# One call for an expert's four inner transposes, slot rows computed ahead of the weight splits, and the gated sum of expert rows on TensorE

## The chip, the cores and the metric

The kernel runs on one core of one Trainium2 chip, in one launch. The metric is the device time of a run in microseconds (us). The time before is 3627.87 us, the median of three runs (3625.42 to 3634.18).

## What is computed

Two layers, each: a modulated RMSNorm, an input projection, token mixing (an RWKV-7 scan, a short convolution, a Fourier mix), an output projection with a gated residual, a second RMSNorm, and a mixture of experts with a gated residual. Layer 0 works on 1280 tokens (256 of context, 1024 latent), layer 1 on the 1024 latent tokens alone; the result is the latent stream after a last RMSNorm. The change touches the mixture of experts:

```python
pg = softmax(h @ router_g_w + router_g_b); pg_top, grp = top_k(pg, 1)          # 4 groups
top_l, top_i = top_k((h @ router_e_w + router_e_b) of that group, 2)          # 8 experts in a group
gates = pg_top * softmax(top_l);  eid = grp * 8 + top_i                        # 2 experts for each token
y[slot] = (silu(xb @ exp_gate[e]) * (xb @ exp_up[e])) @ exp_down[e]            # blocks of 128 rows of one expert
out[token] = sum over its 2 experts of gate * y[slot]
x = x + g2 * out;   at the end: rmsnorm(x, final_g)
```

D_MODEL is 1024 and an expert's width 512, so one expert has 6 MB of float32 weights.

## The kernel before

`trace` runs the layers one after the other: input projection (L397), scan, output projection with the router beside it (`router`, L1276 to L1510), then `experts` (L1513) and `combine` (L1710).

**Float32 accuracy out of faster products.** Every operand of a large product is split into a high part and a rest: `split` writes the high part on ACT (L175) and the rest, source minus high part, on DVE (L176), for some pieces on POOL. A product then takes three passes (`PASS`): high by high, high by rest, rest by high.

**Experts.** The 32 experts of a layer follow one another, with up to 128 rows each. For each, six loads of 1 MB (`load`, L1539, on SP, seven buffers `ld`) bring the weights; `cut` splits them into twelve pieces of 128x1024 in `hl` buffers; a gather on POOL (L1527) brings the expert's rows `xg`; `turn` transposes them on TensorE (L1557, four for each half); `up` makes two products, `pR` and `pU` (L1571, 12 instructions in each of four calls); `act` makes `s` out of them (L1576 on ACT, L1577 and L1578 on DVE); `turned` transposes `s` in four pieces of 128x128 into the PSUM tile `pm` (L1586) and splits the result; `down` makes 24 products (L1595); `out` copies to SBUF (L1601) and scatters the rows to `yb` on POOL (L1602). While an expert computes, the next one's pieces are split and its first `up` stands ahead of this one's `turned`; the next but one's first `turn` stands between `turned` and `down`:

```python
act(x)
if n1:
    up(n1, 0)
    cut(n1, 2, 3, pool=3)
    ask()
turned(x)
if n2:
    turn(n2, 0)
down(x)
```

`in_order` (L158) chains all instructions that are traced inside it, engine by engine, into the order in which they are written (SP is left out); outside it a scheduler orders each engine's instructions from its own estimate. In the first experts of a layer some small router work (`late`, L1498 to L1507) is laid between. Rows beyond 128 of an expert are done by a loop behind the 32 (L1682), which runs once in layer 0; so 65 expert blocks are computed in all.

**Slots.** Which token row stands in which slot is gathered on TensorE into `ids` (L1407, L1408). `primary` (L1440) turns that into the gather and scatter rows `gat` and `sca` by `rows` (L1433 to L1438, five small DVE operations). It is called before `experts`, outside `in_order`. The first gather (L1527) needs `gat`.

**Combine.** For each tile of 128 tokens, ten in layer 0 and eight in layer 1, the two expert rows of a token are loaded as `y0` and `y1` (L1734, L1736). ACT scales `y0` by the first gate (L1737), DVE adds `y1` times the second (L1738), POOL multiplies by the modulation row (L1739), DVE adds the residual (L1740). Then come the norm's square sum (L1742), root (L1744) and reciprocal (L1745). In layer 1 the normed tile is stored (L1747, L1748). In layer 0 the tile is stored (L1750), scaled (L1751), and each pair of tiles goes to `norm1`, which transposes it on TensorE (L307), applies the modulation (L310 on ACT, L313 on DVE) and splits it; the next layer's input projection (L397) begins with all pairs.

## Time and profile before

| | |
|---|---|
| median of three runs | 3627.87 us (3625.42 to 3634.18) |
| the profiled execution | 3623.64 us; span on the core 3621.7 us; 1.9 us lie around it |
| mean granted TensorE clock | 0.906 |
| busy share of the span | PE 85%, PEld 67%, DVE 63%, ACT 52%, POOL 33% |
| DMA | 922 MB, mean 255 GB/s |
| experts, layer 0 / layer 1 | from about 1131 to 1815 us / from about 2916 to 3560 us |
| combine, layer 0 / layer 1 | from about 1819 to 1906 us / from about 3563 us to the end |

PE is TensorE's products, PEld its weight loads, DVE VectorE, ACT ScalarE, POOL GpSimd, SP the queue that issues most transfers. A share of busy time is a mean over stages with different limits, so the stages are read apart, by the views of which rows are copied below. A granted clock of 1.00 is 2.4 GHz, one of 0.50 is 1.2 GHz. A DMA share of 1.00 means that the core's 16 DMA engines are busy all the time.

### The profile page before, as it was taken

How to read it: one execution, taken by the hardware profiler on the slowest of the kernel's cores; microseconds unless marked ns; L12 is line 12 of the kernel's file. 1: busy time of each engine (PE TensorE's matmuls, PEld its weight loads, DVE VectorE, ACT ScalarE, POOL GpSimd, SP SyncE). 2: the span in 40 equal slices, each digit the busy share in tenths (PEclk: the TensorE clock that was granted, in tenths of full speed). 3: DMA queues.
4: the chain of work that ended last, by engine and by line, in shares of the span. 5: the costliest groups of instructions: out<-in, count | busy, mean ns of one | idle time of the engine just before them, and what ended most of it. 6: DMA issues, size and time to landing. Idle time of an engine off the chain costs nothing. (4 is left out here: it accounts for less than half of the span.)

```text
span 3621.7 us, 59282 instructions
## 1 busy us (share of the span) xinstructions
PE 3063.4 (85%) x22308; PEld 2426.6 (67%) x22308; DVE 2281.6 (63%) x3543; ACT 1880.5 (52%) x2838; POOL 1178.0 (33%) x1101
## 2 busy tenths in 40 slices
PE   6998788888997999999829988778878978999992
PEld 3776666676686777777616766556666857777772
DVE  4265566134487888888672665652334778888886
ACT  4343433335344777778652434323343467777783
POOL 0037675211221222222140276743113122233323
PEclk8998888899998999999959988778988989999996
DMA  6677888879746899999667578889795488899995
GB/s 241 207 167 173 185 192 181 246 230 315 260 142 243 334 339 338 365 373 363 257 227 258 144 169 181 176 180 252 240 285 167 133 315 317 331 366 364 360 366 205
DMA packets 708060, 922.35 MB, mean 255 GB/s; under 512 B 335074, under 2 KB 561259, under 8 KB 657852
## 3 DMA queue, kind: packets, MB, share of 16 engines
q1 hardware_dynamic: 669456, 871.05, 75.8%
q0 software_dynamic: 38304, 47.49, 3.9%
q8 instruction: 177, 2.90, 0.3%
q14 instruction: 111, 0.91, 0.1%
q10 hardware_dynamic: 12, 0.00, 0.0%
HBM read 726.92 MB, written 203.23 MB: 257 GB/s over the span
## 5 line engine op out<-in xcount | busy, mean ns | idle before, releaser
L176 DVE TENSOR_TENSOR hl<-ld,hl 128x1024 fp32r<-128x1024 f32 x734 | 869.2, 1228 | 54.2 <-ACT hl L175 44.2
L175 ACT ACTIVATE hl<-ld 128x1024 fp32r<-128x1024 f32 x796 | 798.5, 1052 | 38.4 <-PE pR L1571 21.9
L1571 PE MATMUL pR<-hl,wk 128*128 128x512 f32 x1560 | 455.1, 400 | 0.0
L1571 PE MATMUL pU<-hl,wk 128*128 128x512 f32 x1560 | 446.9, 395 | 0.0
L397 PE MATMUL pb<-hh,wh 128*128 128x512 f32 (+1 forms) x1000 | 393.0, 394 | 10.2 <-ACT wh L175 5.4
L397 PE MATMUL pb<-hl,wh 128*128 128x512 f32 (+1 forms) x1000 | 389.1, 390 | 0.0
L397 PE MATMUL pb<-hh,wl 128*128 128x512 f32 (+1 forms) x1000 | 385.4, 386 | 0.0
L1595 PE MATMUL pA<-hl,wk 128*128 128x512 f32 x1560 | 382.9, 401 | 0.5 <-ACT wk L175 0.5
L1571 PEld LDWEIGHTS pU<-hl,wk 128*128 128x128 f32 x1560 | 294.5, 189 | 68.3
L1595 PEld LDWEIGHTS pA<-hl,wk 128*128 128x128 f32 x1560 | 292.7, 191 | 64.0 <-ACT wk L175 0.7
L1571 PEld LDWEIGHTS pR<-hl,wk 128*128 128x128 f32 x1560 | 288.3, 189 | 60.7 <-ACT wk L175 0.3
L176 POOL TENSOR_TENSOR hl<-ld,hl 128x1024 fp32r<-128x1024 f32 x62 | 184.2, 2971 | 422.4 <-ACT hl L175 422.4
L397 PEld LDWEIGHTS pb<-hh,wh 128*128 128x128 f32 x1000 | 200.2, 200 | 76.8 <-issue 14.1
L1602 POOL DMA_INDIRECT yb<-wk,sca x64 | 94.8, 1482 | 468.2 <-ACT wk L1601 452.1
L1276 PE MATMUL pA<-hl,wk 128*128 128x512 f32 x864 | 226.6, 413 | 7.7 <-POOL wk L176 4.0
L397 PEld LDWEIGHTS pb<-hl,wh 128*128 128x128 f32 x1000 | 201.1, 201 | 37.9 <-issue 10.3
L397 PEld LDWEIGHTS pb<-hh,wl 128*128 128x128 f32 x1000 | 200.2, 200 | 35.2 <-issue 4.6
L1100 POOL DMA_DIRECT2D yD<-yt x72 | 58.0, 805 | 433.7 <-ACT yt L1099 391.6
L1276 PEld LDWEIGHTS pA<-hl,wk 128*128 128x128 f32 x864 | 163.0, 195 | 49.2 <-issue 6.0
L1088 DVE TENSOR_TENSOR tm<-pR,ST 128x256 f32<-128x256 f32 x76 | 32.1, 423 | 249.4 <-PE pR L1083 237.4
L175 ACT ACTIVATE wk<-pm 128x256 fp32r<-128x256 f32 (+1 forms) x195 | 88.8, 455 | 185.6 <-PE pm L1586 169.3
L607 POOL TENSOR_TENSOR gt<-gt,tmp 120x30 f32<-120x30 f32 (+14 forms) x240 | 168.3, 701 | 17.7
(425 smaller groups left out, 5389.6 us busy)
## 6 DMA issues: line engine op xcount, KB each, us to landing
ld<-in_exp_gu SPq DMA_DIRECT2D x260, 1024.0 KB
ld<-in_exp_dn SPq DMA_DIRECT2D x130, 1024.0 KB
st<-rlD SPq DMA_DIRECT2D x80, 512.0 KB
wr<-in_w_in SPq DMA_DIRECT2D x46, 512.0 KB
rlD<-ar SPq DMA_DIRECT2D x64, 320.0 KB
rlD<-X SPq DMA_DIRECT2D x64, 320.0 KB
btD<-bt SPq DMA_DIRECT2D x64, 320.0 KB
st<-abD SPq DMA_DIRECT2D x40, 512.0 KB
```

The costliest lines, as they stand in the source:

```text
L175: nc.scalar.activation(hi, src, AF.Copy)
L176: (eng or nc.vector).tensor_tensor(lo, src, hi.bitcast(F32), op=OP.subtract)
L397: mm = nc.tensor.matmul(ps[:, :n], w[:, k, :], h[:, k, c0:c0 + n], start=(k == 0 and i == 0), stop=(k == KD - 1 and i == 2))
L607: eng.tensor_tensor(gt[:, 0:j, j + 1:32], gt[:, 0:j, j + 1:32], tv, op=OP.add)
L1088: nc.vector.tensor_tensor(tm, RS[:, 1], ST[d], op=OP.add)
L1100: nc.gpsimd.dma_start(self.yD[d][:, ch * C:(ch + 1) * C, :], yt.rearrange("q p d -> q (p d)"))
L1276: nc.tensor.matmul(ps, oo[o][:, k, :], w[k][w_][:, fs], start=(k == 0 and q == 0), stop=(k == KD - 1 and q == 2))
L1571: nc.tensor.matmul(o, x.xT[xi][:, kk, :], w[wi][:, k, :], start=(kk == 0 and i == 0), stop=(kk == KD - 1 and i == 2))
L1595: nc.tensor.matmul(x.y[n], x.h[:, hi_, f, :], dw[wi][:, 0, n * 512:(n + 1) * 512], start=(f == 0 and i == 0), stop=(f == 3 and i == 2))
L1602: nc.gpsimd.indirect_dma_start(out=yb, out_offset=bass.IndirectOffsetOnAxis(ap=x.sca, axis=0), in_=o, in_offset=None, bounds_check=2 * T - ...
```

## The change

Four edits. In `turned` all four transposes are issued first and both splits follow. `primary` is called as the first thing inside `in_order`, so that its operations stand where they are written. At the start of the experts the second expert's first `turn` moves behind the first `up`. In `combine` the gate scaling on ACT, the addition on DVE and the multiplication on POOL go; instead ACT writes two diagonal 128x128 matrices with the gates (identity times gate), TensorE forms the gated sum of `y0` and `y1` as float32 products in PSUM (four of 512 columns for a tile, each sum over two diagonals), and DVE multiplies the PSUM tile by the modulation row.

```diff
             pt = pp.tile([P, 4, P], F32, name="pm")
             x.h = self.wk([P, 2, 4, P], F32R)
+            for f in range(4):
+                nc.tensor.transpose(pt[:, f, :], x.s[:, f * P:(f + 1) * P], self.ident)
             for f2 in (slice(0, 2), slice(2, 4)):
-                for f in range(f2.start, f2.stop):
-                    nc.tensor.transpose(pt[:, f, :], x.s[:, f * P:(f + 1) * P], self.ident)
                 self.split(x.h[:, 0, f2], x.h[:, 1, f2], pt[:, f2])
...
         with self.in_order():
+            primary()
             for e in range(3):
                 xs[e] = slot(e)
...
             turn(x, 0)
             turn(x, 1)
-            turn(xs[1], 0)
             up(x, 0)
             cut(x, 6, 7)
             ask()
+            turn(xs[1], 0)
             cut(xs[1], 0)
...
+        pp = self.tc.alloc_tile_pool(name="cmb", bufs=1, space=PSUM, side="right", reuse_waits="tile")
...
-            nc.scalar.activation(y0, y0, AF.Copy, scale=R["gate"][:, t, 0:1])
-            nc.vector.scalar_tensor_tensor(y0, y1, R["gate"][:, t, 1:2], y0, op0=OP.mult, op1=OP.add)
-            nc.gpsimd.tensor_tensor(y0, y0, rw_[w], op=OP.mult)
+
+            dg = sb.tile([P, 512], F32, name="s2", bufs=N2)[:, :2 * P].rearrange("q (c t) -> q c t", c=2)
+            for c in range(2):
+                nc.scalar.activation(dg[:, c], self.ident, AF.Copy, scale=R["gate"][:, t, c:c + 1])
+            ps = pp.tile([P, D], F32, name="sum", bufs=2)
+            for n in range(2):
+                fs = slice(n * 512, (n + 1) * 512)
+                for c, y in enumerate((y0, y1)):
+                    nc.tensor.matmul(ps[:, fs], dg[:, c], y[:, fs], start=c == 0, stop=c == 1)
+            nc.vector.tensor_tensor(y0, ps, rw_[w], op=OP.mult)
             nc.vector.tensor_tensor(xt, xt, y0, op=OP.add)
...
-        primary()
         k.lp.release()
```

How the change moves instructions is seen at three places. In the rows below a line number is that of the kernel the row belongs to, x3 stands for three such instructions in a row, and [waits DVE_49] for a wait on DVE's semaphore (Activation is ACT, DMASW a transfer that POOL issued).

PE, one expert in the middle of layer 0, before: `pm` takes the transposes of `s`, `pl` those of the rows of the expert after next, `pA` the products of `down`.

```order
L1586 MATMUL pm<-ident,s_13605 128x128 [waits DVE_49]
L1586 MATMUL pm<-ident,s_13605 128x128
L1586 MATMUL pm<-ident,s_13605 128x128 [waits DVE_49]
L1586 MATMUL pm<-ident,s_13605 128x128
L1557 MATMUL pl<-ident,xg 128x128 [waits DMASW7_49]
L1557 MATMUL pl<-ident,xg 128x128 x3
L1595 MATMUL pA<-hl,wk 128x512 [waits Activation_49]
L1595 MATMUL pA<-hl,wk 128x512 x11
```

The same place now:

```order
L1585 MATMUL pm<-ident,s_13605 128x128 [waits DVE_49]
L1585 MATMUL pm<-ident,s_13605 128x128 x3
L1557 MATMUL pl<-ident,xg 128x128 [waits DMASW7_49]
L1557 MATMUL pl<-ident,xg 128x128 x3
L1595 MATMUL pA<-hl,wk 128x512 [waits Activation_49]
L1595 MATMUL pA<-hl,wk 128x512 x3
L1595 MATMUL pA<-hl,wk 128x512 [waits DVE_49]
```

The wait for DVE between the second and the third transpose is gone; a wait for DVE stands at the fifth product of `down` instead.

DVE, the start of the experts of layer 0, as a difference (- before, + now): `rt_ids` and the rows up to `sca` are those that the first gather needs, `hl<-ld` the splits of the first expert's weights.

```order
-L176 TENSOR_TENSOR hl<-ld_10635,hl 128x1024
 L1433 TENSOR_SCALAR rt_z<-rt_ids 128x32
 L1435 TENSOR_SCALAR rt_s<-rt_ids 128x32
-L176 TENSOR_TENSOR hl<-ld_10635,hl 128x1024
 L1436 SCALAR_TENSOR_TENSOR rt_z<-rt_z,rt_ids 128x32
-L176 TENSOR_TENSOR hl<-ld_10637,hl 128x1024
 L1437 TENSOR_TENSOR gat<-rt_z,rt_s 128x32
 L1438 CAST sca<-rt_z 128x32
-L176 TENSOR_TENSOR hl<-ld_10637,hl 128x1024
+L176 TENSOR_TENSOR hl<-ld_10633,hl 128x1024 x2
+L176 TENSOR_TENSOR hl<-ld_10635,hl 128x1024 x2
+L176 TENSOR_TENSOR hl<-ld_10637,hl 128x1024 x2
```

The five operations of `rows` stood among six splits, and now stand ahead of all six.

PE, `combine` of layer 0, now: `sum` takes the products through the diagonals (`s`), `n1ps` the transposes of a pair of tiles by `norm1`.

```order
L1747 MATMUL sum<-y_16763,s_16767 128x512
L1747 MATMUL sum<-y_16765,s_16767 128x512
L1747 MATMUL sum<-y_16784,s_16788 128x512
L307 MATMUL n1ps<-ident,y_16651 128x128 x4
L1747 MATMUL sum<-y_16863,s_16867 128x512
L307 MATMUL n1ps<-ident,y_16672 128x128 x4
L307 MATMUL n1ps<-ident,y_16651 128x128
L307 MATMUL n1ps<-ident,y_16672 128x128
```

Before, only the transposes stood here. Now the products of the third tile, the first product of the fourth and the first one of the fifth stand ahead of or among the transposes of the first pair.

## Rows read from the trace of the kernel before

**Rows 1.** Windows: stretch, us, busy us (instructions) per engine, PEclk, DMA share, GB/s.

```profile
3200.00:3300.00 100.00, 95.34 (x446) 77.82 (x445) 86.77 (x91) 80.42 (x102) 36.01 (x17) 1.00 0.95 360
...
1500.00:1600.00 100.00, 95.34 (x440) 76.71 (x439) 85.61 (x89) 79.44 (x100) 27.94 (x17) 1.00 0.96 369
...
3000.00:3100.00 100.00, 90.72 (x421) 73.70 (x420) 88.06 (x122) 73.18 (x92) 26.58 (x14) 0.98 0.86 320
...
1362.00:1368.00 6.00, 6.00 (x30) 4.88 (x29) 5.05 (x9) 5.31 (x6) 2.50 (x2) 1.00 1.01 380
...
1820.00:1905.00 85.00, 22.74 (x80) 13.98 (x80) 68.12 (x88) 48.56 (x98) 37.80 (x19) 0.50 0.64 241
3564.00:3621.00 57.00, 0.00 (x0) 0.00 (x0) 42.22 (x32) 21.32 (x33) 23.20 (x8) 0.50 0.68 258
```

**Rows 2.** Waits of PE in layer 1's experts: us in total, times, longest us.

```profile
PE pm L1586 <- DVE wk L176: 32.3, 32, 1.8
```

**Rows 3.** Timeline, a steady expert of layer 1: start us, us, engine, line, operation [idle before].

```profile
3246.42 0.69 DVE L1577 TENSOR_TENSOR s<-s,pR 128x512 f32<-128x512 f32 x1 [0.16 <-ACT s L1576]
...
3249.02 0.38 PE L1586 MATMUL pm<-ident,s 128*128 128x128 f32 x2
3249.44 0.38 ACT L175 ACTIVATE wk<-pm 128x256 fp32r<-128x256 f32 x1 [1.16 <-PE pm L1586]
3249.86 0.42 DVE L176 TENSOR_TENSOR wk<-pm,wk 128x256 fp32r<-128x256 f32 x1 [0.82 <-ACT wk L175]
...
3250.34 0.44 PE L1586 MATMUL pm<-ident,s 128*128 128x128 f32 x2 [0.93 <-DVE wk L176]
...
3250.61 0.60 PE L1557 MATMUL pl<-ident,xg 128*128 128x128 f32 x4
...
3250.97 1.86 PE L1595 MATMUL pA<-hl,wk 128*128 128x512 f32 x7
```

**Rows 4.** Timeline of POOL: scatters of neighbouring experts, layer 1, then layer 0.

```profile
3200.95 1.59 POOL L1602 DMA_INDIRECT yb<-wk,sca  x1 [6.59 <-ACT wk L1601]
...
3219.94 1.58 POOL L1602 DMA_INDIRECT yb<-wk,sca  x1 [6.66 <-ACT wk L1601]
...
1671.98 1.50 POOL L1602 DMA_INDIRECT yb<-wk,sca  x1 [6.80 <-ACT wk L1601]
...
1691.22 1.51 POOL L1602 DMA_INDIRECT yb<-wk,sca  x1 [6.79 <-ACT wk L1601]
```

**Rows 5.** Timeline, start of layer 0's experts, DVE.

```profile
1131.58 0.18 DVE L1408 TENSOR_TENSOR rt_ids<-rt_ids,pm 128x32 f32<-128x32 f32 x1
...
1135.69 0.18 DVE L1438 CAST sca<-rt_z 128x32 int32<-128x32 f32 x1
```

**Rows 6.** Timeline of PE, start of layer 0's experts.

```profile
1145.43 1.11 PE L1557 MATMUL pl<-ident,xg 128*128 128x128 f32 x4 [15.36 <-DMA xg<-hx,gat]
...
1149.30 1.09 PE L1557 MATMUL pl<-ident,xg 128*128 128x128 f32 x4 [1.90 <-DMA xg<-hx,gat]
1150.04 1.63 PE L1571 MATMUL pR<-hl,wk 128*128 128x512 f32 x3
```

**Rows 7.** Groups of lines in layer 0's combine: busy us, mean ns | idle before.

```profile
L1751 DVE TENSOR_SCALAR y<-wk,r 128x1024 f32<-128x1024 f32 x10 | 15.7, 1567 | 0.1
...
L1738 DVE SCALAR_TENSOR_TENSOR y<-y,gate,y 128x1024 f32<-128x1024 f32 x10 | 14.5, 1447 | 7.3 <-DMA y<-yb 7.3
```

**Rows 8.** Groups of lines in layer 1's combine.

```profile
L1747 DVE SCALAR_TENSOR_TENSOR wk<-wk,r,xg 128x1024 f32<-128x1024 f32 x8 | 16.2, 2030 | 0.3
L1738 DVE SCALAR_TENSOR_TENSOR y<-y,gate,y 128x1024 f32<-128x1024 f32 x8 | 14.2, 1780 | 18.2 <-DMA y<-yb 18.1
```

**Rows 9.** Timeline of DVE in layer 1's combine, its last operation.

```profile
3616.70 1.28 DVE L1747 SCALAR_TENSOR_TENSOR wk<-wk,r,xg 128x1024 f32<-128x1024 f32 x1
```

**Rows 10.** Line L238 by form: float32 products of 512 columns, min/median/max ns.

```profile
L238 PE MATMUL ps<-w,cc x64: 591/902/1057, 13.7 to 41.3; 128*2 128x512 f32 x64
```

**Rows 11.** Window of PE, the first products of layer 0's experts.

```profile
1149.30:1155.00 5.70, 5.70 (x16) 0.50 0.39 155
```

More of the change, by code (lines that the diff above doesn't have):

```diff
@@ L1510, in router, with experts @@
         return route, primary, finish
-    def experts(self, l, hx, yb, R, finish, xmid, t0):
+    def experts(self, l, hx, yb, R, primary, finish, xmid, t0):
         nc, tc, a = self.nc, self.tc, self.a
@@ L1755, in combine @@
                 t0, xs = t + 1, []
+        pp.release()
 def dft(n, scale):
@@ L1906, in trace @@
             k.outproj(l, last, xs[l], xmid, hx, readout, ots, route)
-        primary()
         k.lp.release()
         k.lp = tc.alloc_tile_pool(name="lde", bufs=1, reuse_waits="tile")
-        xts = k.experts(l, hx, yb, R, finish, xmid, 2 if last else 0)
+        xts = k.experts(l, hx, yb, R, primary, finish, xmid, 2 if last else 0)
         k.scp.release()
```

## The prediction

> **What bounds the kernel now.** I read the windows first, to see which engine is full in which stage. In the steady experts PE is busy 95% of the time at a granted clock of 1.00, and the transfers have a share of 0.95 to 0.96 at 360 GB/s (layer 1) and 369 GB/s (layer 0); in the first experts of a layer, where router work is laid between, it is 0.86 and 320 GB/s [rows 1]. So the experts are bound by PE, with the transfers close behind. The two combines are another matter: PE has a clock of 0.50, the transfers stand at 0.64 and 0.68, and DVE is busy 68.1 of 85 us and 42.2 of 57 us [rows 1]; its chain from tile to tile sets the end.
>
> Then the waits, for what PE's idle time is: in layer 1's experts PE waited for DVE at L1586 32 times, once in each expert, 32.3 us in all [rows 2]. Then the timeline of one expert shows the step itself [rows 3]: two transposes at 3249.02, ACT's split at 3249.44, DVE's at 3249.86, and only then, at 3250.34, the other two, though `s` had long been there. The first product of `down` starts at 3250.97, 1.95 us after the first transpose. The period of an expert is 18.99 us in layer 1 (3219.94 - 3200.95) and 19.24 us in layer 0 [rows 4]. Last, the timelines of the two starts and the groups of lines of the two combines [rows 5 to 8].
>
> **The inner transposes.** Four transposes in a row take 0.60 us [rows 3]. Now both splits wait behind them: four transposes, then ACT's split (0.38), with two handovers of some 0.04 (3249.82 to 3249.86 is one): about 1.06 us from the first transpose to the first product of `down`. The transposes of L1557 (0.60) stand on PE meanwhile and end earlier. 1.95 - 1.06 = 0.89 us saved for each expert. If the first split is released after two transposes it starts as before, at 0.42, and ends 0.80 after the first transpose, but the eight transposes keep PE until about 0.9: 1.05 us saved. DVE's rest (0.42) is wanted first by the fifth product, four products of 0.27 (1.86 for seven, [rows 3]) later, so at 2.1; it is there at about 1.5, covered by 0.6 us. I take 0.89 for 65 blocks: **-58 us**; the ends are -68, and, if everything waits on, 0.
>
> What is late next? The transfers. An expert moves 360 x 18.99 = 6.8 MB in layer 1 and 369 x 19.24 = 7.1 MB in layer 0. At the new periods, 18.1 and 18.35, that asks for 378 and 387 GB/s. A window of 6 us shows 380 at a share of 1.01 [rows 1]. With 380 as the most, layer 1 gets through and layer 0 needs 18.68 us, 0.33 us more for each of some 20 steady experts: **+7 us**.
>
> The Trainium skill, on its page "DMA: Bandwidth & Descriptors", Specifications, gives about 358 GB/s as a core's share of the memory. By that figure a layer 1 expert could not be under 19.1 us, and the steady experts would gain nothing. The trace disagrees already, with 369 over 100 us [rows 1].
>
> **The start of the experts.** `ids` is done at 1131.58 and `sca` at 1135.69, with DVE splits between [rows 5]. The five small operations take some 0.18 us at most each, and now follow one another, and `ids` no longer stands behind two splits: `sca` at about 1131.2, some 4.5 us earlier; without the last effect 3.2. The first gather and all behind it move with it, since PE's first `turn` waited 15.36 us for that gather [rows 6]. The six splits that come later on DVE (about 1.2 us each) end at about 1138.6, before PE's first product wants them at 1143. Moving the second `turn` takes its wait (1.90) and its own 0.74 off the front of the first product (from 1149.30 to 1150.04, [rows 6]); the wait is now covered by twelve products. In sum 4 to 7 us a layer; I take 6, twice: **-12 us**. The weight loads are in SP's queue and don't move ahead.
>
> **Combine, layer 0.** On DVE, L1738 goes (14.5 us) and a product with a PSUM tile of 1024 columns comes. Its price is bounded by twice the row for 512 columns, 2 x 0.69 = 1.38 us [rows 3], and by 1.28, the operation from SBUF [rows 9]; I take 1.3: 13 us for ten tiles, so -1.5. POOL's multiplication goes too. Beside it DVE is slow: L1747 takes 2.03 us on average and 1.28 where POOL is idle [rows 8, 9]. If L1751 (1.57 on average, [rows 7]) loses the same 0.75, that is -7.5. ACT trades a pass over 1024 columns for two of 128, and is not what is waited for. Sum **-9 us**; ends -15 and what the products cost.
>
> That is the added work: a tile has four float32 products, and the trace has such products of 512 columns as two records each, 0.59 us at the high clock, 1.06 at the low [rows 10]. Without overlap a tile is 8 x 0.59 = 4.7 us; at the 0.27 spacing of the products of `down` [rows 3] 2.1. I take the middle, 3.4, and 6.8 at the low clock. At the high clock ten tiles are 34 us, beside 22.7 of transposes (at the low clock, [rows 1]) in a stage of 85: hidden. The change puts three tiles' products in a row at the start, and TensorE's first products of the experts ran 5.7 us at 0.50 before the clock rose [rows 11]; so I expect the clock to rise here within the first two tiles.
>
> **Combine, layer 1.** DVE is the chain. L1738 goes (14.2), the PSUM product comes (8 x 1.3 = 10.4), L1747 drops from 2.03 to 1.28, -6 [rows 8, 9], and the addition between them gains a little. DVE falls by 10 to 12 us; the first tile's products, at the low clock, put 6.8 us where DVE's 1.3 stood, but DVE waited 18.1 us for `yb` there [rows 8], and those transfers run on meanwhile. **-10 us**; ends -14 and the case below.
>
> **The sum.** -58 + 7 - 12 - 9 - 10 = -82 us, against the profiled 3623.64: 3541.6. The median of the runs shown stands 4.2 us above that execution, so I forecast **3546 us**. About 0.3%, 11 us, is what a measurement of this kernel can tell from no change.
>
> **Rivals.**
> *The transfers take over.* If each layer can't move more over long stretches than the 360 and 369 GB/s that it shows [rows 1], the 40 steady experts gain nothing, and only the 24 early ones (share 0.86) and the last block keep 0.89: -22 in place of -51, 3575 us. For it: a share of 0.95 leaves little. Against: 380 in the short window. Chance 0.14.
>
> *TensorE stays at the low clock in the combines.* Then layer 0's needs 10 x 6.8 + 23 = 91 us of PE and some 5 for the first data: 96 against 85, +11 in place of -9. Layer 1's needs 8 x 6.8 = 54, and about 13 for the first data and the last tile's norm and store: 67 against 58, +9 in place of -10. 3546 + 39 = 3585 us; for one of the two alone 3566. For it: PE was at 0.50 through both stages, though layer 0's had 22.7 us of transposes [rows 1].
>
> The Trainium skill, "TensorE: Matmul & The Clock Gate", HAM oscillation, speaks against this part of the change: bursts of products with waits for data between them fall back to the low clock each time. By it both combines would be this rival's. The trace bears it out only as far as the 0.50 goes, with no products in either stage. Chance 0.16.
>
> *The wait only moves.* If the first product of `down` waits for DVE's rest as well, or for the second half's split, it starts at about 1.5 or 1.9 after the first transpose in place of 1.06, and the expert keeps some 0.2 us on average of the two: 13 in place of 51, 3584 us. For it: the added wait at the fifth product. Against: 0.6 us of cover. Chance 0.05.
>
> *Slower.* PE takes its instructions in order, and in layer 0's combine the products of the third tile and the first ones of the fourth and fifth now stand ahead of or among the first pair's transposes. If those wait for loads that need buffers which the norm behind the transposes frees, products and norm run one after the other at the low clock: up to 18 x 6.8 = 122 us bare. -58 + 7 - 12 + 122 = +59, 3687 us. It decides from about half of the products bare (63 of 122 us). Against: only the first product of the later tile stands ahead, and `y0` has five buffers. Chance 0.03.
>
> **Chances.** Forecast 0.62; the others as given. All but the last are faster by over 11 us. Faster 0.95, same 0.02, slower 0.03. The range goes down to where the experts save 68, the starts 14 and the combines 15 and 10 with no loss to the transfers, -107 in place of -82, or 3521; since not all come together, 3522. Up it takes in the three rivals that give 3575 to 3585: 3590.
>
> **What would show it.** Right: no idle PE between transposes at L1585 and a first product of `down` about 1.06 us behind the first; periods of 18.1 us in layer 1 and near 18.5 in layer 0, at a share near 1.00; the first gather near 1131.5; the clock over 0.9 in most of both combines, and DVE's operations there at 1.3 us. Wrong: periods unchanged with PE waiting for `hl` splits that wait for `ld`; a clock of 0.50 in the combines, with DVE waiting for `sum`; or combines longer than 86 and 58 us.

## The result, and the profile after

The change takes the kernel from 3626.64 us (median of 4 runs, 3623.01 to 3634.18) to **3517.65 us** (median of 4, 3517.36 to 3518.51): a ratio of 0.9697, with a 95% interval of 0.968 to 0.9714. The profiled span falls from 3621.7 to 3515.6 us, the mean granted clock rises from 0.906 to 0.926. Faster, as forecast, but by 109 us where 82 were forecast, and 4 us below the range.

To see where the time came from, I cut both spans at the same events: the last product of L1407 (the slots), the first of L1571 (the experts), the first load of `y0`, the first of L397 in layer 1.

| stage, us | forecast | before | after | difference |
|---|---|---|---|---|
| start and layer 0 up to its slots | 0 | 1129.7 | 1132.2 | +2.5 |
| slots to first expert, layer 0 | -6 | 20.3 | 12.8 | -7.5 |
| experts, layer 0 | with layer 1's | 669.5 | 647.4 | -22.1 |
| experts, layer 1 | -51 for both | 628.3 | 610.6 | -17.7 |
| combine, layer 0 | -9 | 86.2 | 76.5 | -9.7 |
| layer 1, first L397 to last L1407 | 0 | 1008.9 | 972.3 | **-36.6** |
| slots to first expert, layer 1 | -6 | 20.3 | 12.8 | -7.5 |
| combine, layer 1 | -10 | 58.5 | 51.0 | -7.5 |
| sum | -82 | 3621.7 | 3515.6 | -106.1 |

The six edited stages gave 72.0 us of the 82 forecast (7.5 + 22.1 + 17.7 + 9.7 + 7.5 + 7.5). A third of the gain, 36.6 us, came in the middle of layer 1, where no line was edited: input projection, scan, Fourier mix, output projection, router.

First the windows of the changed kernel, as in [rows 1]: stretch, us, busy us (instructions) of PE, PEld, DVE, ACT and POOL, granted clock, DMA share, GB/s. The stretches are steady experts of layer 1 and of layer 0, early experts, and the two combines.

```profile
3200.00:3300.00 100.00, 99.78 (x465) 81.38 (x464) 88.81 (x94) 83.38 (x107) 35.72 (x17) 1.00 0.98 377
...
1500.00:1600.00 100.00, 99.82 (x458) 80.33 (x457) 88.92 (x93) 80.99 (x104) 36.15 (x17) 1.00 0.99 385
2900.00:3000.00 100.00, 93.38 (x423) 75.18 (x422) 92.11 (x120) 72.29 (x93) 25.11 (x15) 0.97 0.87 320
1792.40:1868.00 75.60, 56.17 (x158) 26.59 (x158) 54.54 (x89) 43.84 (x106) 7.94 (x8) 0.84 0.73 271
3468.00:3515.00 47.00, 31.77 (x64) 12.68 (x64) 29.76 (x32) 16.34 (x37) 0.00 (x0) 0.86 0.78 297
```

In the steady experts PE is busy 99.8% where it was 95.3%: its wait is gone, and the transfers followed, at 377 and 385 GB/s. In the early experts the transfer rate is 320 GB/s as before: nothing was gained there. The combines have a clock of 0.84 and 0.86 where it was 0.50.

The step itself, in a steady expert of layer 1 (timeline: start us, us, engine, line, operation, idle before), answers to [rows 3]:

```profile
3253.72 0.60 PE L1585 MATMUL pm<-ident,s 128*128 128x128 f32 x4
3254.15 0.60 PE L1557 MATMUL pl<-ident,xg 128*128 128x128 f32 x4
3254.35 0.38 ACT L175 ACTIVATE wk<-pm 128x256 fp32r<-128x256 f32 x1 [1.38 <-PE pm L1585]
3254.77 0.42 DVE L176 TENSOR_TENSOR wk<-pm,wk 128x256 fp32r<-128x256 f32 x1 [1.04 <-ACT wk L175]
3254.79 5.77 PE L1595 MATMUL pA<-hl,wk 128*128 128x512 f32 x24
```

ACT starts at 3254.35, after all four transposes and not after two; the first product of `down` stands 1.07 us behind the first transpose (1.06 forecast), and all 24 run through. The scatters give the period [rows 4]: two of layer 1, then two of layer 0.

```profile
3207.69 1.64 POOL L1602 DMA_INDIRECT yb<-wk,sca  x1 [6.12 <-ACT wk L1601]
...
3225.82 1.65 POOL L1602 DMA_INDIRECT yb<-wk,sca  x1 [6.12 <-ACT wk L1601]
...
1611.12 1.63 POOL L1602 DMA_INDIRECT yb<-wk,sca  x1 [6.19 <-ACT wk L1601]
...
1629.52 1.65 POOL L1602 DMA_INDIRECT yb<-wk,sca  x1 [6.18 <-ACT wk L1601]
```

18.13 us (18.99 before) and 18.40 (19.24): 0.86 and 0.84 a block, 0.89 forecast.

The start of layer 0's experts, DVE [rows 5] and PE [rows 6]:

```profile
1132.62 0.19 DVE L1408 TENSOR_TENSOR rt_ids<-rt_ids,pm 128x32 f32<-128x32 f32 x1 [0.47 <-PE pm L1407]
...
1133.39 0.17 DVE L1438 CAST sca<-rt_z 128x32 int32<-128x32 f32 x1
...
1143.17 1.11 PE L1557 MATMUL pl<-ident,xg 128*128 128x128 f32 x4 [10.59 <-DMA xg<-hx,gat]
1145.03 1.64 PE L1571 MATMUL pR<-hl,wk 128*128 128x512 f32 x3
...
1148.61 0.60 PE L1557 MATMUL pl<-ident,xg 128*128 128x128 f32 x4
```

`sca` follows `ids` by 0.77 us where it took 4.11, and the second expert's `turn` stands behind the first products, with no wait. From the slots to the first product it is 12.8 us instead of 20.3.

The combines by groups of lines (busy us, mean ns of one | idle before), layer 0, then layer 1, beside [rows 7, 8]:

```profile
L1748 DVE TENSOR_TENSOR y<-sum,xg 128x1024 f32<-128x1024 f32 x10 | 12.2, 1220 | 5.8 <-PE sum L1747 5.7
...
L1760 DVE TENSOR_SCALAR y<-wk,r 128x1024 f32<-128x1024 f32 x10 | 8.5, 849 | 0.2
...
L1756 DVE SCALAR_TENSOR_TENSOR wk<-wk,r,xg 128x1024 f32<-128x1024 f32 x8 | 10.2, 1281 | 0.1
L1748 DVE TENSOR_TENSOR y<-sum,xg 128x1024 f32<-128x1024 f32 x8 | 9.8, 1222 | 24.6 <-PE sum L1747 24.6
```

The product from PSUM takes 1.22 us (1.3 taken), and with POOL's multiplication gone (POOL busy 7.94 us in layer 0's window in place of 37.80, and 0.00 in layer 1's) the scaling falls from 1567 to 849 ns (forecast -0.75), the last operation from 2030 to 1281 (forecast 1.28). The wait for `yb` of 18.1 us has become one of 24.6 for `sum`.

### The profile page after: what moved, and what is told of

It is laid out like the page before. It is cut to its first block, busy times and chain, and to the rows that moved or that the text cites. A ratio compares the mean times of both kernels' runs of the same rounds, so it can differ in the third digit from the quotient of the medians.

```text
span 3515.6 us, 59528 instructions
## 1 busy us (share of the span) xinstructions
PE 3123.8 (89%) x22452; PEld 2447.4 (70%) x22452; DVE 2274.8 (65%) x3543; ACT 1852.3 (53%) x2856; POOL 1140.5 (32%) x1083
## 5 line engine op out<-in xcount | busy, mean ns | idle before, releaser
L176 DVE TENSOR_TENSOR hl<-ld,hl 128x1024 fp32r<-128x1024 f32 x734 | 892.0, 1267 | 39.4 <-ACT hl L175 37.3
L1571 PE MATMUL pR<-hl,wk 128*128 128x512 f32 x1560 | 455.5, 400 | 0.0
L1571 PE MATMUL pU<-hl,wk 128*128 128x512 f32 x1560 | 446.5, 394 | 0.0
L397 PE MATMUL pb<-hh,wh 128*128 128x512 f32 (+1 forms) x1000 | 392.0, 393 | 4.1 <-ACT r L430 1.7
L397 PE MATMUL pb<-hh,wl 128*128 128x512 f32 (+1 forms) x1000 | 385.9, 386 | 6.5 <-DVE wl L176 6.5
L397 PE MATMUL pb<-hl,wh 128*128 128x512 f32 (+1 forms) x1000 | 386.4, 387 | 0.0
L1571 PEld LDWEIGHTS pU<-hl,wk 128*128 128x128 f32 x1560 | 294.2, 189 | 68.1
L1571 PEld LDWEIGHTS pR<-hl,wk 128*128 128x128 f32 x1560 | 288.1, 189 | 61.4 <-ACT wk L175 0.8
L176 POOL TENSOR_TENSOR hl<-ld,hl 128x1024 fp32r<-128x1024 f32 x62 | 174.1, 2809 | 369.8 <-ACT hl L175 369.8
L397 PEld LDWEIGHTS pb<-hh,wh 128*128 128x128 f32 x1000 | 199.9, 200 | 67.6 <-issue 11.5
L397 PEld LDWEIGHTS pb<-hh,wl 128*128 128x128 f32 x1000 | 200.1, 200 | 42.3 <-DVE wl L176 6.8
L397 PEld LDWEIGHTS pb<-hl,wh 128*128 128x128 f32 x1000 | 200.3, 200 | 37.5 <-issue 9.6
L1088 DVE TENSOR_TENSOR tm<-pR,ST 128x256 f32<-128x256 f32 x76 | 32.0, 422 | 235.0 <-PE pR L1083 216.6
L561 PE MATMUL ps<-ar,bk 64*128 64x128 f32 x1280 | 124.5, 334 | 55.9 <-DVE X L566 22.8
```

The source lines that it names most:

```text
L176: (eng or nc.vector).tensor_tensor(lo, src, hi.bitcast(F32), op=OP.subtract)
L397: mm = nc.tensor.matmul(ps[:, :n], w[:, k, :], h[:, k, c0:c0 + n], start=(k == 0 and i == 0), stop=(k == KD - 1 and i == 2))
L561: mm = nc.tensor.matmul(ps[:, e, c], bk[h, c0 + c].rearrange("q s t -> q (s t)"), ar[h, :, c0 + c, :], start=True, stop=True)
L1088: nc.vector.tensor_tensor(tm, RS[:, 1], ST[d], op=OP.add)
L1571: nc.tensor.matmul(o, x.xT[xi][:, kk, :], w[wi][:, k, :], start=(kk == 0 and i == 0), stop=(kk == KD - 1 and i == 2))
```

## The experiments

Two theories for the 36.6 us. *Order:* an edit can make the scheduler order layer 1's untouched middle in another way, and the order of before was a long one. *Resources:* what the edits free (PE, DVE, POOL or buffers, or an earlier end of the combine) lets the middle run faster. By the first, the length of the middle goes with its order, whichever edit was made; by the second it goes with the edit. The other questions: why the early experts gained nothing, and whether the clock bounds the combines.

### The parts alone

Each is one part of the change on the kernel before. **only_T**: in `turned` the two transposes inside the loop are taken out and four stand ahead of it.

```diff
+            for f in range(4):
+                nc.tensor.transpose(pt[:, f, :], x.s[:, f * P:(f + 1) * P], self.ident)
             for f2 in (slice(0, 2), slice(2, 4)):
-                for f in range(f2.start, f2.stop):
-                    ...
```

> Only the four inner transposes ahead of their split; all else as before. Stages by the profile: experts of layer 0 last 669.5 us before and 647.4 in the changed kernel, those of layer 1 628.3 and 610.6; the middle of layer 1 (first L397 to last L1407) 1008.9 and 972.3. Theory (order): layer 1's middle changed length because the scheduler put its instructions in another order; here that order is the one of before on DVE, ACT and POOL, so the middle stays at 1009 within 4 us; the experts give -22 and -18 us as in the changed kernel, the early ones of each layer (beside router work) nearly nothing; total about -39 us. Rival (edits together): the early experts gain nothing because the other edits are in; alone this edit gives 0.85 us in all 65, -55 us.

Measured: 3587.85 us, ratio 0.9888 (0.9867 to 0.9908). Experts 647.0 and 608.6, as in the whole change; the middle 1006.9, as before.

**only_M**: one moved call.

```diff
             turn(x, 1)
-            turn(xs[1], 0)
             up(x, 0)
             cut(x, 6, 7)
             ask()
+            turn(xs[1], 0)
```

> Only the move of the second expert's first turn behind the first up. Theory (order): gaps before the experts 20.3 us to about 18 in both layers; the experts as before; but the scheduler's order of layer 1's middle differs from before on all five engines, so its length can move by tens of us either way from 1008.9, though no code of it changed. Rival (resources): the middle got shorter because the combine left POOL and DVE freer or TensorE faster for it; with the combine as before it stays at 1009 within 4 us, and the total is -4 us.

Measured: 3588.9 us, ratio 0.9889 (0.9868 to 0.991), as much as all of `turned`. The slots to the first expert take 17.7 and 17.9 (before 20.3), the experts 668.3 and 631.1, the combine 87.7 as before, and the middle **974.5**: -34.4 us. One call, moved by a few places in the experts, is worth what the whole change is worth in a stage that doesn't contain it, and by the trace DVE, ACT and POOL run the middle here in the order of the whole change, operation by operation. Resources can't explain that: nothing that layer 1's middle uses was freed.

**only_S**: `primary()` as the first thing inside `in_order`.

```diff
         with self.in_order():
+            primary()
...
-        primary()
```

> Only the slot rows computed ahead of the splits. Gap before the experts 20.3 us to about 16 in both layers (12.8 with the moved turn, 17.8 with the turn alone); experts and combines as before. Theory (order): the middle of layer 1 has an order of its own and some length between 970 and 1010. Rival: the moved turn, not its order, shortened the middle in the run with that move alone; then the middle is 1009 here.

Measured: 3599.68 us, ratio 0.9923 (0.9898 to 0.9948). The starts are 15.9 and 15.6, so -4.4 and -4.7 (forecast 3.2 to 4.5 for this part); the middle 986.0.

**only_C0** and **only_C1**: the diagonal sum in one layer alone.

```diff
+            if not last:    # only_C1: if last
+                dg = ...
+                nc.vector.tensor_tensor(y0, ps, rw_[w], op=OP.mult)
+            else:
                 nc.scalar.activation(y0, y0, AF.Copy, scale=R["gate"][:, t, 0:1])
```

> Only layer 0's combine through diagonals; layer 1's combine as before. Combine of layer 0 from 86.2 to about 76.5 us. Theory (order): the middle of layer 1 has an order of its own here (neither that of before nor that of the changed kernel) and a length of its own, unlike 972.3 by more than 5 us. Rival (resources): it is 972 as in the changed kernel, total -46 us.

Measured: 3603.46 us, ratio 0.9936 (0.9913 to 0.996). The combine itself takes 84.7, only 1.5 less; the middle 982.8, 26.1 less. PE's order in the combine is another than in the whole change:

```profile
1845.31 12.03 PE L1746 MATMUL sum<-y,s 128*128 128x512 f32 x22
...
1868.49 6.37 PE L1746 MATMUL sum<-y,s 128*128 128x512 f32 x8
...
1874.92 3.60 PE L1746 MATMUL sum<-y,s 128*128 128x512 f32 x8
```

22 records of products stand in one piece where the whole change has 6 and 16 with transposes between. DVE's product waited 17.6 us for `sum`, where it waited 5.7 in the whole change:

```profile
L1747 DVE TENSOR_TENSOR y<-sum,xg 128x1024 f32<-128x1024 f32 x10 | 12.2, 1222 | 17.8 <-PE sum L1746 17.6
```

That looks like the forecast's "slower" rival (products ahead of the pair's transposes), but it isn't where the 8 us between this combine (84.7) and that of the whole change (76.5) went. Of the 17.6 us, 9.6 lie at the first tile, where DVE waited as long in the whole change, there for ACT's `wh` (9.98 us). Counted from the first load of `y0`, DVE's products of the fourth to the ninth tile start 0.9 to 1.5 us later than in the whole change, that of the tenth 5.5 us later (72.2 against 66.7). So most of the 8 us came behind the ninth tile, and why is not settled.

> Only layer 1's combine through diagonals. All five engines have the order of before in layer 1's middle. Theory (order): middle 1009 within 3 us; combine of layer 1 from 58.5 to about 51 us; total -7 to -8 us. Rival (chance): the length of the middle wanders from run to run by itself, then it is off from 1009 here by over 5 us with the same order.

Measured: 3627.53 us, ratio 0.9982 (0.9963 to 1.0002): not told from no change. Its profiled execution took 16061 us, so its stages can't be read, and it was run again.

> Layer 1's combine through diagonals alone, once more, for its stages. The order of the middle is that of before on all engines: middle 1009 within 3 us by the order theory; combine of layer 1 from 58.5 to 51 us.

Measured: 3621.12 us (one run). The combine is 48.0, so -10.5; all stages ahead within 5 us of before, the middle 1012.4 among them, with its instructions in the order of the kernel before.

**only_TSM**: the whole change without the diagonal sum.

> The changed kernel with both combines as before. Gaps before the experts 12.8 us, experts 647 and 611 us, combines 86 and 58 us. Theory (order): layer 1's middle has once more an order of its own on all five engines, so a length that is not bound to 972.3 nor to 1008.9, though the combine is that of before; total 3533 us plus what the middle has over 972. Rival (resources of the combine): the combine of before gives the middle of before, 1009; total 3570.

Measured: 3541.88 us, ratio 0.9746 (0.9707 to 0.9784); experts 647.9 and 609.6, starts 12.8 and 13.1, middle 982.6.

Taken together, the parts' gains by ratio (41, 40, 28, 23 and 7 us) sum to 139 where the whole change gives 110: M, S and C0 each hold a reordered middle (34, 23 and 26 us), and the whole can have one such middle only.

### Whether the middle's length is its order

Layer 1's scan (first to last L1061) lies in the middle. By form: count, min/median/max ns, first and last start. Before:

```profile
L397 PE MATMUL pb<-hh,wh x448: 277/389/796, 1905.7 to 2576.5; 128*128 128x512 f32 x123, 128*128 128x256 f32 x27
...
L1061 PE MATMUL pR<-st,st x640: 222/222/370, 2475.0 to 2752.4; 128*64 128x64 f32 x160
...
L1407 PE MATMUL pm<-rt_bo,rt_ro x32: 190/334/419, 2852.3 to 2914.6; 128*128 128x32 f32 x32
```

only_M:

```profile
L397 PE MATMUL pb<-hh,wh x448: 277/389/796, 1903.4 to 2562.4; 128*128 128x512 f32 x123, 128*128 128x256 f32 x27
...
L1061 PE MATMUL pR<-st,st x640: 222/222/370, 2462.3 to 2708.6; 128*64 128x64 f32 x160
...
L1407 PE MATMUL pm<-rt_bo,rt_ro x32: 190/334/420, 2818.2 to 2877.9; 128*128 128x32 f32 x32
```

The scan takes 277.4 us before and 246.3 in only_M (245.8 in the whole change, 2427.4 to 2673.2): 31 of the 34 us. The instructions are the same and their medians too. More of them ran at the lower clock before (granted clock 0.88 in the scan, 0.93 in only_M), but the clock isn't the reason: the changed kernel, run once more (after_again below), had the scan at nearly the same granted clock as before (0.89 and 0.88) and was 27 us shorter. The scan's window (columns as in [rows 1]), before, then in after_again:

```profile
2475.03:2752.43 277.40, 221.59 (x3556) 178.88 (x3557) 89.94 (x211) 113.98 (x278) 48.20 (x68) 0.88 0.89 263
...
2429.48:2679.71 250.23, 220.09 (x3535) 176.35 (x3537) 82.36 (x197) 109.07 (x266) 47.29 (x69) 0.89 0.95 275
```

Two neighbouring steps show how the order costs time (L1088 is a step of the scan, L743 the first half of the Fourier branch); DVE, before:

```profile
2593.65 0.42 DVE L1088 TENSOR_TENSOR tm<-pR,ST 128x256 f32<-128x256 f32 x1 [0.90 <-PE pR L1083]
...
2602.79 0.69 DVE L743 TENSOR_TENSOR k<-lw 128x511 f32<-128x511 f32 x1 [7.94 <-DMA st<-abD]
...
2609.85 0.69 DVE L743 TENSOR_TENSOR k<-lw 128x511 f32<-128x511 f32 x1 [5.00 <-DMA lw<-fD]
...
2610.59 0.41 DVE L1088 TENSOR_TENSOR tm<-pR,ST 128x256 f32<-128x256 f32 x1
```

and after:

```profile
2545.13 0.43 DVE L1088 TENSOR_TENSOR tm<-pR,ST 128x256 f32<-128x256 f32 x1 [1.13 <-PE pR L1083]
...
2551.67 0.42 DVE L1088 TENSOR_TENSOR tm<-pR,ST 128x256 f32<-128x256 f32 x1 [5.34 <-PE pR L1083]
```

16.9 us against 6.5 between the 18th step and the next: before, DVE had the Fourier branch's work laid between, waited 7.94 and 5.00 us for its transfers, and came to the step late (no wait ahead of it); after, DVE was there first and waited 5.34 for PE. Up to the 18th step the two scans stand within some 5 us of each other, counted from their first product, and there within 1 (118.7 and 117.7 us). A gap of about 30 us, for the branch's second half, comes in both, but behind the 23rd step before and behind the 27th after. The 28th step stands at 203.3 us before and at 191.6 after, the 36th at 245.6 and 227.1, the 38th and last at 274.4 and 239.0: the difference grows from 11.7 to 18.5 to 35.4 us.

On DVE the branch's first half (L743) stands behind 18 steps and its second (L899) behind 23 to 25 in the kernel before, only_T and only_C1_again, with scans of 277 to 284 us; behind 19, 21 and 27 to 31 in the seven runs with scans of 241 to 250 (the whole change, once more, only_M, only_C0, only_TSM, late_dve, pool_later); but only_S, with 18 and 23 to 27, has 252. So that place alone doesn't set it.

**before_late_readout** and **after_late_readout** were meant to keep the output projection's first half (`readout`, of which POOL, ACT and DVE rows lie among the last scan steps) out of the scan:

```diff
-E_AT, F_AT = (32, 3), (2, 3)
+E_AT, F_AT = (1000, 3), (2, 3)
```

> The kernel before, with one number changed: no tile's readout (L1139 to L1190) is begun while the scan still runs, in both layers; the same work is done behind it. Theory (readout in the way): with the order of before, the readout's first operations stand on DVE and ACT ahead of the scan's last steps and wait there for POOL and a transfer (L1160 8.2 us, L1163 8.7 and 7.1 us), so layer 1's scan (first to last L1061) takes 277.4 us where nine other orders have 241 to 256; without them it is 256 us or less, and some 10 to 15 us of readout come behind it; the whole middle falls from 1009 to 985 to 1000. Rival (the scan's loads): the 30 us are lost to late transfers of vE and abD at the scan's start and middle; then the scan stays above 268 us, and the middle does not fall below 1009.

> The changed kernel with the same one number changed. Its scan of layer 1 takes 246 to 250 us already. Theory (readout in the way): there is little to win in it, at most 10 us, and the readout behind it costs as much or more: the middle stays at 975 or grows by up to 15 us. Rival: the middle falls by as much as in the kernel before.

Measured: 3618.27 us, ratio 0.9961 (0.9949 to 0.9974), scan 275.4, middle 1006.2; and 3549.04 us, ratio 0.9775 (0.9754 to 0.9797), scan 285.5, middle 1003.8. The edit didn't do what it was meant to: ahead of the scan's last step DVE has 18 operations of the readout in both runs, as many as in the kernel before; the changed kernel has 3. So neither theory was tested, but the second run speaks for the first one: with 18 in place of 3 the scan of the changed kernel got 40 us longer. Over all fifteen profiles the five with 18 have scans of 275 to 286 us, the ten with 3 have 241 to 265. The scan's last steps on DVE, before:

```profile
2720.63 0.42 DVE L1088 TENSOR_TENSOR tm<-pR,ST 128x256 f32<-128x256 f32 x1 [2.06 <-PE pR L1083]
...
2730.03 0.69 DVE L1160 TENSOR_REDUCE mean<-ld 128x8 f32<-128x512 f32 x1 [8.20 <-POOL ld L1158]
...
2730.84 0.42 DVE L1088 TENSOR_TENSOR tm<-pR,ST 128x256 f32<-128x256 f32 x1
...
2749.48 0.42 DVE L1088 TENSOR_TENSOR tm<-pR,ST 128x256 f32<-128x256 f32 x1
```

From the third last step (2720.63) to the last (2749.48) it is 28.85 us before and 11.85 in the change: 17 of the 35.4 us. That the readout's place causes them is likely, not shown: no run moved it alone.

**before_fill4** begins the Fourier branch four steps later:

```diff
-            if F_AT[0] * b // F_AT[1] > F_AT[0] * (b - 1) // F_AT[1]:
+            if b >= 4 and F_AT[0] * b // F_AT[1] > F_AT[0] * (b - 1) // F_AT[1]:
```

> The kernel before, with the second half of the Fourier branch (fill, L883 to L971) begun four scan steps later in program order, in both layers. In DVE's order of layer 1 its operations at L899 then stand behind 25 to 29 scan steps in place of 23 to 26 (27 and 31 in the changed kernel). Theory (the Fourier halves stand too early among the scan steps): the 30 us gap in which the scan waits for that half comes behind more steps, and the scan (277.4 us) falls by 10 to 20 us; the middle falls below 1000. Rival (not this half: the first half at L743, behind 18 steps here as before, and the order of the rest): the scan stays at 270 us or more.

Measured: 3643.35 us, ratio 1.0024 (1.0004 to 1.0043). The scan did fall, by 12 us to 265.4, but 11 of them came back between the scan and the output projection (17.7 us where 6.6 stood), the middle ended at 1004.6, and layer 0 lost 20. Half right: time moved mostly from one side of the scan's end to the other. And the 12 us aren't the branch's alone, since the readout moved too (3 operations ahead of the last step in place of 18).

What fifteen profiles show as a whole, middle in us. The orders were read from the traces, line by line for each engine. The programs of each of the first three rows run the same sequence on ACT and POOL, and on DVE but for one pair of neighbours; PE's records, some of which are missing, agree but for such gaps and neighbours.

| order of layer 1's middle | programs | middle |
|---|---|---|
| that of before | before, only_T, only_C1_again | 1008.9, 1006.9, 1012.4 |
| that of the whole change | the change, once more, only_M, late_dve | 972.3, 979.3, 974.5, 973.7 |
| a third | only_C0, only_TSM | 982.8, 982.6 |
| one of its own each, no edit inside the middle | pool_later, only_S, norm_by_products | 975.7, 986.0, 1002.3 |
| one of its own each, with an edit in it | after_late_readout, before_fill4, before_late_readout | 1003.8, 1004.6, 1006.2 |

The middle goes with the order: runs of one order agree within 7 us, whatever their edits, and the orders lie up to 40 apart. only_C0 and only_TSM have no edit in common, and in the same order the same middle; only_M has one edit of the change, its order and its length; norm_by_products has every part of the change, another order, and a middle 30 longer. That what the edits free pays for the 36.6 us is excluded by these. Which instructions of the order cost the time is settled in part: the Fourier branch among the scan's steps, where DVE waits for its transfers, and probably the readout among the last ones.

**after_again** is the changed kernel once more, for the wander of a stage by itself.

> The changed kernel once more, unaltered: how far its stages wander by themselves. Layer 1's middle 972 within 4 us, gaps 12.8, experts 647 and 611; the combine of layer 0, which held two clocks, is the stage that may differ most from 76.5.

Measured: 3525.37 us; middle 979.3 (+7), combine 1 49.0 (-2), all others within 1.3. So a stage's difference of some 7 us in the middle, and 2 in the experts and combines, tells nothing. The start up to layer 0's slots, which the parts above don't touch, lay anywhere between 1124.9 (only_TSM) and 1138.4 us (only_T).

### The early experts

In the first experts of a layer the period went from 19.44 to 19.38 us in layer 1 and from 19.68 to 19.58 in layer 0. Timeline of one in the whole change (the two splits `hl<-ld` are of the next expert's weights):

```profile
2969.24 2.38 POOL L176 TENSOR_TENSOR hl<-ld,hl 128x1024 fp32r<-128x1024 f32 x1 [5.68 <-ACT hl L175]
...
2969.72 2.98 DVE L176 TENSOR_TENSOR hl<-ld,hl 128x1024 fp32r<-128x1024 f32 x1
...
2971.38 1.21 PE L1595 MATMUL pA<-hl,wk 128*128 128x512 f32 x4
...
2972.62 0.41 DVE L176 TENSOR_TENSOR wk<-pm,wk 128x256 fp32r<-128x256 f32 x1
...
2973.09 4.87 PE L1595 MATMUL pA<-hl,wk 128*128 128x512 f32 x20 [0.50 <-DVE wk L176]
```

Four products run, and the fifth waits 0.50 us for DVE's rest, which stands behind a weight split of 2.98 us that ran beside POOL's. Before, in the same place, DVE began first and POOL paid:

```profile
3051.56 1.22 DVE L176 TENSOR_TENSOR hl<-ld,hl 128x1024 fp32r<-128x1024 f32 x1
3051.74 3.25 POOL L176 TENSOR_TENSOR hl<-ld,hl 128x1024 fp32r<-128x1024 f32 x1 [6.58 <-ACT hl L175]
```

Two edits of the changed kernel test it. **pool_later** puts POOL's piece behind `turned`:

```diff
-                    cut(n1, 2, 3, pool=3)
+                    cut(n1, 2)
                     ask()
                 turned(x)
+                if n1:
+                    cut(n1, 3, pool=3)
```

> The changed kernel, with the one split on POOL issued behind the splits of turned in place of ahead of them. Theory: in the early experts (router work between) DVE's split of a weight piece ran 2.98 us beside POOL's in place of 1.22, and so ate what the transposes gave; now they shrink from 19.4 to about 18.6 us in layer 1 and from 19.6 to 18.9 in layer 0, -13 to -16 us in the experts of both layers together. Rival: the collision only moves to the splits behind down, where DVE is 89% busy, and the periods stay or grow, in the steady experts too (18.13 and 18.40 now). Layer 1's middle has an order of its own and may differ by tens of us either way.

Measured: 3550.06 us, ratio 0.9775 (0.9732 to 0.9817), so some 0.8% longer than the change (0.9775 against 0.9697). The steady period is 18.80 us where the change has 18.13: the collision went to the steady experts.

**late_dve** gives that piece to DVE in the experts 2 to 13 alone, behind `turned`:

```diff
-                    cut(n1, 2, 3, pool=3)
+                    cut(n1, 2, *(3,) * (not 2 <= e <= 13), pool=3)
                     ask()
                 turned(x)
+                if n1 and 2 <= e <= 13:
+                    cut(n1, 3)
```

> The changed kernel; only in experts 2 to 13 of each layer the split that POOL made goes to DVE, behind the splits of turned. Theory (DVE beside POOL): DVE's split of 2.98 us is 1.22 again there, the fifth product of down waits for nothing, and the early experts' period falls from 19.39 to 18.6 us in layer 1 and from 19.58 to 18.9 in layer 0, the steady ones stay at 18.13 and 18.40: -7 to -9 us in each layer. Rival (DVE is full there): DVE's added 1.22 us for each expert keeps the period at 19.4 or lengthens it. The middle of layer 1 may get another order, so the total may differ from the stages' sum by up to some 15 us either way.

Measured: 3517.27 us, ratio 0.9686 (0.966 to 0.9713), no better than the change. Here the collision is gone:

```profile
2973.96 1.22 DVE L176 TENSOR_TENSOR hl<-ld,hl 128x1024 fp32r<-128x1024 f32 x1
2974.20 0.63 PE L1585 MATMUL pm<-ident,s 128*128 128x128 f32 x4 [0.24 <-DVE s L1578]
...
2975.30 5.77 PE L1595 MATMUL pA<-hl,wk 128*128 128x512 f32 x24
```

All 24 products run through, and the early experts take 19.02 us in both layers: -0.36 and -0.56. But some blocks among them are longer than in the change (in layer 0 22.17, 22.10 and 22.07 us in place of 21.51, 21.11 and 21.08), and the layers' experts end as in the change (648.7 and 608.1). So in a regular early block the collision held about half of the 0.89 that was missing. The rest is argued: DVE has 1.22 us more to do for each of these experts, and between 2930 and 3060 us PE waited for `s` from DVE 7.9 us in six waits, where it was 3.1 in two in the change.

### The clock in the combines

**norm_by_products** writes `norm1`'s transposes as products, on the changed kernel:

```diff
-                nc.tensor.transpose(ps[:, i * P:(i + 1) * P], xn[:, k * P:(k + 1) * P], self.ident)
+                nc.tensor.matmul(ps[:, i * P:(i + 1) * P], xn[:, k * P:(k + 1) * P], self.ident, start=True, stop=True)
```

> The changed kernel; the norm's transposes (L307) are made as float32 products with the identity in place of transposes. Theory (clock): in layer 0's combine the granted clock falls to 0.50 after each stretch in which PE only transposed and waited, so eight products take 6.4 us in place of 3.6; with products in place of transposes the clock stays above 0.95 from the third tile on, the eight-product rows all take 3.6 us, and the combine falls from 76.5 to about 70 us. Rival (idle time, not the kind of work): PE waits as often for DVE and ACT as before, the clock goes up and down as before (mean 0.83), and the combine stays at 76 or grows, since a product of 128 columns has two records and a transpose one.

Measured: 3535.52 us, ratio 0.9737 (0.9708 to 0.9766). The window of layer 0's combine:

```profile
1787.00:1863.00 76.00, 62.42 (x241) 36.89 (x241) 55.76 (x92) 46.07 (x112) 8.92 (x9) 0.90 0.71 270
```

The clock rose from 0.84 to 0.90 and the stage stayed at 76.4 us (76.5 in the change). PE had more to do as well (62.42 us busy, 56.17 in the change), so the run alone doesn't part the two; but DVE waited 5.5 us for `sum`, as in the change (5.7). The clock isn't what bounds layer 0's combine. What this kernel lost, it lost in the middle (1002.3).

## Why the prediction was right or wrong

**The step that failed** is the one that wasn't made: the sum went over the edited lines, and everything else stood in it as nothing. The forecast was made of -58 + 7 - 12 - 9 - 10; layer 1's middle has no term, though an edit ahead of it can make the scheduler order all of it anew, as the parts M, S and C0 did and T did not. It brought -36.6 us, more than the whole distance from the forecast (3546) to the result (3517.65). The order of before happened to be a long one: the five other orders that came from edits outside the middle, the change's among them, are 7 to 37 us shorter. So this part of the gain is luck and no merit of the edits. That the order changes could have been known ahead; its size and sign could be had only from such runs, so the term should have been an open one, with wide bounds on both sides. Without it the edited stages gave 72 of the 82 us, a time inside the range. The range had a slip of its own: its lower end takes 10 us for layer 1's combine, where the text above it allows 14. With 14 it would be 3517, and would have taken in the result for a wrong reason.

**The inner transposes: mechanism right, count wrong.** 1.07 us from the first transpose to the first product (1.06), 0.86 and 0.84 off each steady block (0.89). But the regular ones of the 24 early blocks gave 0.06 to 0.10 each, not 0.89. The forecast's cover of 0.6 us for the fifth product was worked out from a split of DVE that comes right behind ACT's; there DVE is in a weight split of 2.98 us. That is the rival "the wait only moves", true of the early blocks alone. 40 x 0.85 + 24 x 0.08 = 36 of the 39.8 us that the experts gave, and the rest lies in a few longer early blocks (two of layer 0 fell from 23.5 to 21.1 us); -51 was forecast for the experts.

**The transfers didn't take over.** The 7 us set aside weren't lost: layer 0's 385 GB/s over 100 us is above the 380 taken as the most. The Trainium skill, "DMA: Bandwidth & Descriptors", Specifications, gives some 358 GB/s for a core; the trace disagrees, with 385 sustained. An estimate from that figure has the steady experts at 19.1 us and more; they take 18.13 and 18.40. The rival that put the limit at 360 to 369 falls with it; at a share of 0.99 a next gain on PE in layer 0 may find it, which no run tried.

**The starts: mechanism right, size a little over.** -15 for two, -12 forecast, and 7.5 a layer where 4 to 7 was the range: -4.4 and -4.7 from `primary` alone, -2.6 and -2.4 from the moved `turn`, and they add up (7.0 and 7.1 of 7.5).

**The combines: right in size.** -9.7 (forecast -9) and -7.5 (-10; 49.0 and 48.0 us in other runs of the same code, so -9 to -11). Product from PSUM 1.22 us, a tile's four products 3.60 us at the high clock (forecast 3.4), and the relief of DVE from POOL as expected. The low-clock rival is half right in its sign: the clock fell and rose several times. The Trainium skill, "TensorE: Matmul & The Clock Gate", HAM oscillation, says that bursts with waits between them fall back; the trace agrees, with one tile's products at 6.37 us in only_C0 (granted clock 0.56 there) and a mean of 0.84 and 0.86, but not with the price that the rival put on it (+39): in layer 0 DVE waited for `sum` 5.7 us in all.

**Slower** was given 0.03, and no run shows it: in only_C0, with 22 records of products in one piece, DVE's products of the tiles from there to the ninth came 0.9 to 1.5 us later than in the whole change.

## What to carry to other kernels

Where a scheduler orders the program, an edit can be an edit of everything behind it: compare the order of the untouched stages as well, and where it changes give them a term with both signs; here edits outside a stage moved it by 7 to 37 us, at most more than either layer's experts gained. Read a result by stages cut at the same events in both traces before explaining its total, and take a part of the change alone before believing that the parts add up. Look in the trace whether an edit did what it was meant to: the two that should have moved the readout did not. When a wait is moved from one engine to another, look at what the second engine does in every phase of the loop, not only in the steady one.

## What the runs showed of the hardware that was not expected

- Transfers of 1 MB loads ran at 385 GB/s for 100 us at a share of 0.99, against 369 before at 0.96.
- A DVE split of 128x1024 took 1.22 us or 2.98 us beside the same POOL operation. In the two places shown, the engine that began first was the one that was held less: with DVE first (3051.56 against 3051.74) DVE took 1.22 and POOL 3.25; with POOL first (2969.24 against 2969.72) POOL took 2.38 and DVE 2.98. Over the experts of the changed kernel, the 47 such DVE splits that began ahead of an overlapping one on POOL took 1.22 each; of the 24 that began while POOL's ran, 21 took 2.0 to 3.4 and three 1.22.
- A DVE product that reads 128x1024 from PSUM took 1.22 us, no longer than L1749's addition of two such tiles from SBUF (1.22; and 1.28 for the operation of [rows 9]).
